# Order of a hybrid mixer's small work: two-source vector forms, parameter rows earlier, weight splits after products, output transposes last, and the first expert pass moved ahead of a gather

## The chip, the cores and the metric

The kernel runs on one core of one Trainium2 chip. The metric is device microseconds of one execution. Its engines are TensorE (PE), VectorE (DVE), ScalarE (ACT), GpSimd (POOL) and SyncE (SP, which issues the large transfers).

## The reference, cut to what matters

One layer of a decoder block for 256 tokens, with 16 learned meta tokens in front (272 rows) and a width of 1024.

```python
h = layer_norm(concat([meta, x]))                      # 272 x 1024
proj = h @ w_in                                        # 1024 x 5640 columns
dn_qkv, dn_z, dn_b, dn_a, sb_qkv, gates = split(proj)
dn_qkv = silu(causal_depthwise_conv(dn_qkv, w))        # 4 heads of 128
beta = sigmoid(dn_b); g = -exp(a_log) * softplus(dn_a + dt_bias)
o_dn = rms_norm(gated_delta_rule_chunked(q, k, v, beta, g)) * silu(dn_z)
o_sb = stick_breaking_attention(sq, sk, sv)            # 8 heads of 64
merged = sig(gA) * (o_dn @ w_branch_dn) + sig(gB) * (o_sb @ w_branch_sb)
h = layer_norm(alpha * h + merged @ w_out)
# MoE: top-1 of 4 groups, top-2 of its 8 experts (32 experts, ff 256)
y = sum over chosen e of combine_e * (silu(h @ gate_e) * (h @ up_e)) @ down_e
return layer_norm(alpha * h + y)[:, 16:]
```

All is float32. The weights are 23 MB of `w_in`, 8 MB of branch and output weights and 96 MB of expert weights (3 MB an expert).

## The kernel before, in words

**The mixer's projection** is 44 groups of 128 columns of `w_in`. `project` runs them in the order of a list: the convolved keys (columns 512 on, groups 0 to 3), the queries and keys of the stick-breaking attention (2056 and 2568 on, groups 4 to 11), the convolved queries (0 on, 12 to 15) and values (1024 on, 16 to 19), the stick-breaking values (3080 on, 20 to 23), z (1536 on, 24 to 27) and the gates (3592 on, 28 to 43). A float32 product is made of three products of rounded halves (`mm3`, L237 to L239): hi with hi, hi with lo, lo with hi. So each group is 8 x 3 matmuls of 128 x 272 or 256, and each weight block is split first (`load_split`): an SP transfer of 0.5 MB into a ring of three raw buffers (L231), a cast on ACT for the hi half (L232), a subtraction on POOL for the lo half (L233; on DVE for three of the first groups) into a ring of WB = 3 buffers of pairs. The activations get the same two halves `hTh` and `hTl` in the first stage (L213 to L217).

**Woven into the groups** are chains of small work, generators that hand over at each `yield`: `delta_net` (the gating numbers beta and g, two chunks' local matrices and a block inversion by doubling, `invert`, then `scan_state` for chunk 0 and chunk 1), `stick_breaking`, the turning of its values, and `parameter_rows`. `weave` takes a step of each chain at a rate per two k-blocks of a group. In the mixer PE and POOL run their instructions in the order in which the program makes them; ACT, DVE and SP are ordered by the tile scheduler. All of them run in order once they are ordered.

In `invert`, for each size n of 4, 8, .., 128 POOL masks a matrix (`mb4c`, .., L488), PE multiplies (`x4c`, L507), ACT casts the result (`xo4c`, L509), and PE goes on with `y4c` and `z4c` (L513, L516). At the end of `scan_state`, the output rows `o` get their norm: sums of squares on ACT (L710), `sso` on DVE (L712 to L714), a power on POOL (L715), one more product on DVE (L716), the scaling on ACT (L718), and then PE transposes them (`poT`, L724) for the branch product.

`parameter_rows` fills `lnr`, `RB` and a selection matrix `self_`: eight POOL instructions (L828 to L835), 12 small transfers on SP (L838), then a scaling on DVE (L839), three casts on ACT (`sel` L840, `RB` L841, `lnh` L842) and a subtraction on DVE (L843). The mixer does not use the result; the second half of the kernel does (L849).

**After the mixer** come the branch products, `w_out`, the layer norm, the router, and 8 units of 4 experts. `gate_up(u)` (L1340) multiplies up to QC slots of each expert, a second pass under `tc.If(most > QC)` takes the rest where an expert has more tokens; `down(u)` (L1389) follows, then the scatter. SP streams the expert weights through rings of buffers: `load_gu` (L889, 2 MB an expert) and `load_dn` (L896, 1 MB an expert). Between the first unit's `gate_up` and its `If` stands the gathering of the second half of the experts' input (`gather(1, ..)` L1195 and `gathered`), and behind the `If` the loads of experts 7 to 10.

Of the kernel before, what the change touches and what calls it, by code (L numbers as in the profile page):

```python
# [19 lines left out]
KT = 8  # L20
# [58 lines left out]
def block_kernel(ctx: ExitStack, tc: tile.TileContext, io, out, dbg=None):  # L79
# [58 lines left out]
    V.memset(one1, 1.0)  # L138
    half = ht.tile([P, HD], F32, name="half")
# [66 lines left out]
    for k in range(KT):  # L206
# [225 lines left out]
    def gating():  # L432
# [6 lines left out]
        V.tensor_scalar_mul(xin[:, 0, :], bb, -1.0)  # L439
# [8 lines left out]
        V.tensor_scalar_add(beta, xin[:, 0, :], 1.0)  # L448
# [3 lines left out]
        V.tensor_scalar_add(zz, u, 2.0)  # L452
# [5 lines left out]
        V.tensor_scalar_mul(poly, z2, 1.0 / 17.0)  # L458
# [3 lines left out]
        V.tensor_scalar_mul(poly, poly, 2.0)  # L462
# [12 lines left out]
        V.tensor_scalar_mul(nedec, dec[:, 0, :], -1.0)  # L475
# [65 lines left out]
    def meta(box):  # L541
# [3 lines left out]
        V.tensor_copy(kTm.rearrange("p (h t) -> p h t", h=HD), qkv[:, 4:8, :NM])  # L545
# [6 lines left out]
        V.tensor_scalar_add(ssm, ssm, RMS_EPS)  # L552
# [31 lines left out]
        V.tensor_copy(vTm.rearrange("p (h t) -> p h t", h=HD), qkv[:, 8:12, :NM])  # L584
# [19 lines left out]
    def local(c, box):  # L604
# [3 lines left out]
        Aall = mx.tile([P, HD, P], F32, name=f"Aall{c}", tag="gtmp", bufs=2)  # L608
# [9 lines left out]
        Es = mx.tile([P, HD, P], F32, name=f"Es{c}", tag="gtmp", bufs=2)  # L618
# [12 lines left out]
        V.tensor_scalar_add(ssk, ssk, RMS_EPS)  # L631
# [24 lines left out]
        V.tensor_scalar(rq, rq, RMS_EPS, float(P), op0=ALU.add, op1=ALU.mult)  # L656
# [15 lines left out]
    def scan_state(c, st, box):  # L672
# [19 lines left out]
        o = mx.tile([P, HD, P], F32, name=f"o{c}", tag="gtmp", bufs=2)  # L692
# [21 lines left out]
        V.tensor_scalar(sso, sso, 1.0 / P, RMS_EPS, op0=ALU.mult, op1=ALU.add)  # L714
# [10 lines left out]
        of = mx.tile([P, HD, P], F32, name=f"of{c}", tag="gtmp", bufs=2)  # L725
# [17 lines left out]
    def delta_net():  # L743
# [80 lines left out]
    def parameter_rows():  # L824

        for _ in range(32):
            yield
# [34 lines left out]
    weave(project(20), (svc, 1.0), (dn, R3), (sbr, R4), (parameter_rows(), 1.0))  # L862
# [272 lines left out]
    load_dn(4, 5)  # L1135
# [315 lines left out]
    def four(u):  # L1451
# [156 lines left out]
```

## Time and profile before

| | us |
|---|---|
| three runs | 544.2, 544.8, 541.4 |
| median | 544.2 |
| profiled execution | 538.66, span 536.9 |
| mean granted TensorE clock in it | 0.922 |

| engine | busy share of the span |
|---|---|
| PE | 86% |
| DVE | 44% |
| ACT | 34% |
| POOL | 32% |

The mixer's 44 groups fill the first 240 us or so of the span, the branches, `w_out`, norms and router lie up to about 300 us, and the experts behind. Up to some 320 us PE is rarely without work and the DMA engines are about half busy; behind it the DMA engines are at their full rate nearly to the end and PE waits for weights now and then. Every row has the start in us (in the time line), the duration, the engine, the line of the kernel, what is written and read, and in square brackets the idle time ahead of it with what ended it. In a table of windows the clock is a share of full speed: 1.00 is 2.4 GHz and 0.50 is 1.2 GHz.

### The profile page before, as it was taken

The numbers are of one execution on the slowest core, as the hardware profiler recorded it, in microseconds if no ns is written. First come the engines' busy times: TensorE is split into PE (matmuls) and PEld (weight loads), VectorE is DVE, ScalarE is ACT, GpSimd is POOL, SyncE is SP. The second block draws the span as 40 slices with busy tenths as digits, with TensorE's granted clock in tenths as the row PEclk, the third lists the DMA queues.
The fourth block names the chain that finished last, engine by engine and source line by source line (L and its number), as shares of the span: only waits on it lengthen the run. The fifth ranks groups of instructions, "written<-read, shape, count | busy, mean of one in ns | idle before, by whom it ended". The sixth has DMA issues, their size and how long they took to land. (4 is left out here: it accounts for less than half of the span.)

```text
span 536.9 us, 8673 instructions
## 1 busy us (share of the span) xinstructions
PE 463.5 (86%) x3301; PEld 328.6 (61%) x3301; DVE 238.2 (44%) x518; ACT 183.9 (34%) x382; POOL 172.7 (32%) x154
## 2 busy tenths in 40 slices
PE   7897999999999978997998888988879888667881
PEld 3697999999997877997876763533222222122330
DVE  5874645665296653039976736120220212110116
ACT  2453546436556365543443312120110202100310
POOL 6594698756544634738132100000000000000002
PEclk9697999999998997999999898889889898878886
DMA  8553344333441612797898958999999999999942
GB/s 210 126 151 86 79 117 109 89 92 108 117 110 49 159 42 78 207 305 270 306 338 336 399 234 336 419 418 418 419 420 420 417 419 418 417 415 419 410 196 79
DMA packets 74581, 136.33 MB, mean 254 GB/s; under 512 B 9857, under 2 KB 59154, under 8 KB 62242
## 3 DMA queue, kind: packets, MB, share of 16 engines
q1 hardware_dynamic: 72640, 134.26, 68.9%
q10 hardware_dynamic: 1890, 1.39, 0.8%
q8 instruction: 32, 0.52, 0.4%
q14 instruction: 19, 0.16, 0.1%
HBM read 133.54 MB, written 2.10 MB: 253 GB/s over the span
## 5 line engine op out<-in xcount | busy, mean ns | idle before, releaser
L233 POOL TENSOR_TENSOR ws_in<-wr_in,ws_in 128x1024 fp32r<-128x1024 f32 x41 | 99.4, 2429 | 64.6 <-ACT ws_in L232 64.3
L237 PE MATMUL pj<-hTh,ws_in 128*128 128x256 f32 (+1 forms) x352 | 109.3, 311 | 1.2 <-DVE hTh L213 0.7
L238 PE MATMUL pj<-hTl,ws_in 128*128 128x256 f32 (+1 forms) x352 | 103.1, 293 | 0.7 <-DVE hTl L217 0.7
L239 PE MATMUL pj<-hTh,ws_in 128*128 128x256 f32 (+1 forms) x352 | 102.6, 292 | 0.0
L1340 PE MATMUL pg<-gu,xs 128*32 128x512 f32 x640 | 77.6, 605 | 8.9 <-DMA gu<-expert_w_up 5.2
L1565 POOL TENSOR_SCALAR rs<-mv 128x1 f32<-128x1 f32 x2 | 0.4, 221 | 229.8 <-DVE mv L1564 229.8
L237 PEld LDWEIGHTS pj<-hTh,ws_in 128*128 128x128 f32 x352 | 69.2, 197 | 3.5 <-issue 1.0
L238 PEld LDWEIGHTS pj<-hTl,ws_in 128*128 128x128 f32 x352 | 69.3, 197 | 1.7 <-DVE hTl L217 1.7
L239 PEld LDWEIGHTS pj<-hTh,ws_in 128*128 128x128 f32 x352 | 69.1, 196 | 0.0
L1389 PE MATMUL py<-dn,hd 128*32 128x512 f32 x320 | 54.1, 802 | 11.9 <-DMA dn<-expert_w_down 6.9
L1340 PEld LDWEIGHTS pg<-gu,xs 128*32 128x32 f32 x640 | 31.0, 111 | 51.0 <-issue 45.5
L232 ACT CAST ws_in<-wr_in 128x1024 fp32r<-128x1024 f32 x44 | 45.9, 1044 | 3.0 <-DMA wr_in<-w_in 3.0
L1393 DVE TENSOR_TENSOR yy<-py,yy 128x512 fp32r<-128x512 f32 x20 | 13.8, 692 | 68.9 <-ACT yy L1392 61.7
L1365 DVE TENSOR_SCALAR sc<-pt,smod 128x256 fp32r<-128x256 f32 x10 | 4.8, 484 | 88.2 <-PE pt L1364 88.2
L1389 PEld LDWEIGHTS py<-dn,hd 128*32 128x32 f32 x320 | 13.2, 138 | 43.8 <-issue 27.2
L1401 PE MATMUL y<-yy,sc 128*128 128x512 f32 x80 | 24.5, 423 | 5.6 <-ACT yy L1392 3.0
L1392 ACT CAST yy<-py 128x512 fp32r<-128x512 f32 x20 | 11.7, 587 | 51.2 <-PE py L1389 51.2
L1401 PEld LDWEIGHTS y<-yy,sc 128*128 128x128 f32 x80 | 13.5, 188 | 22.7 <-ACT yy L1392 7.4
L1371 ACT ACTIVATE gs<-pg 128x256 f32<-128x256 f32 x10 | 3.8, 384 | 68.7 <-PE pg L1340 68.7
L314 DVE SCALAR_TENSOR_TENSOR qkv<-pj,cols,qkv 128x271 f32<-128x271 f32 (+2 forms) x36 | 17.9, 497 | 9.9 <-ACT qkv L312 9.2
L955 POOL TENSOR_TENSOR h<-h,gb 128x512 f32<-128x512 f32 x8 | 12.9, 1643 | 12.9 <-ACT gb L952 12.9
L771 DVE TENSOR_TENSOR_SCAN kp<-kp,one 128x144 f32<-128x144 f32 (+1 forms) x16 | 12.8, 842 | 7.2 <-ACT kp L766 7.2
(535 smaller groups left out, 806.6 us busy)
## 6 DMA issues: line engine op xcount, KB each, us to landing
gu<-expert_w_gate SPq DMA_DIRECT2D x32, 1024.0 KB
gu<-expert_w_up SPq DMA_DIRECT2D x32, 1024.0 KB
dn<-expert_w_down SPq DMA_DIRECT2D x32, 1024.0 KB
wr_in<-w_in SPq DMA_DIRECT2D x44, 512.0 KB
wr_o<-w_out SPq DMA_DIRECT2D x8, 512.0 KB
wr_w_branch_dn<-w_branch_dn SPq DMA_DIRECT2D x4, 512.0 KB
wr_w_branch_sb<-w_branch_sb SPq DMA_DIRECT2D x4, 512.0 KB
h<-x SPq DMA_DIRECT2D x2, 512.0 KB
```

Of the source, the lines that this page charges most:

```text
L232: A.copy(wh, raw)
L233: (sub or V).tensor_sub(wl, raw, f32(wh))
L237: T.matmul(pt, lh, rh, start=first, stop=False)
L238: T.matmul(pt, lh, rl, start=False, stop=False)
L239: T.matmul(pt, ll, rh, start=False, stop=last)
L314: V.scalar_tensor_tensor(y[:, s:], pt[:, :L - s], ccol(3 - s, r + j), y[:, s:], op0=ALU.mult, op1=ALU.add)
L771: V.tensor_tensor_scan(k_, k_, bc(one1, [P, n]), 1.0, op0=ALU.mult, op1=ALU.mult)
L955: G.tensor_tensor(x_, x_, gb, op=op)
L1340: T.matmul(pgd[u, part][c, :], xsd[u, part][:, k, c], raw[e][0][:, :, k, :], start=k == 0, stop=k == KT - 1)
L1389: T.matmul(py[c, :], hd[(u + part) % 2][:, r, c], raw[e][1][:, r, n * 512:(n + 1) * 512], start=r == 0, stop=r == 1)
L1393: V.tensor_sub(yy[:, 1, :], py, f32(yy[:, 0, :]))
L1401: T.matmul(y[t][n], sct[(u + part) % 2][:, t * P:(t + 1) * P], yy[:, p_, :], start=False, stop=p_ == 1 and part == 0 and u == NQ - 1)
```

## The change

1. A helper `with_scalar` writes copies, casts and operations with one scalar as `scalar_tensor_tensor` with a broadcast column of zeros as second source; eleven places of the mixer on DVE use it or a like form with a column of constants. Two copies of 128 x 64 (`kTm`, `vTm`) go from DVE to ACT.
2. `parameter_rows` starts with group 12 and not with group 32. Its POOL instructions and transfers come 20 groups earlier, and 100 yields (25 groups) stand between them and its DVE and ACT instructions, which the scheduler is free to place earlier.
3. `project` makes the split of group i+2 behind the products of group i and not ahead of them.
4. `scan_state` ends with the scaling of `o`; transposing it is a function of its own, `out_turned`, called for both chunks behind the two scans. The ring `gtmp` has three buffers and not two.
5. In the first unit of experts the `If` with the second pass, and the loads of experts 7 to 10, stand ahead of the second half's gathering. A slot buffer of that pass lies in the buffer of expert 5's down weights, whose load moves from ahead of expert 6 to behind expert 7.

```diff
+    def with_scalar(out, x, a, op):
+        V.scalar_tensor_tensor(out, x, a, bc(zero[:x.shape[0]], list(x.shape)) if len(x.shape) == 2 else bc(zero[:x.shape[0], :, None], list(x.shape)), op0=op, op1=ALU.add)
...
-            V.tensor_copy(hTh[:, k, :], hf)
+            with_scalar(hTh[:, k, :], hf, 0.0, ALU.add)
...
+    def splits(n):
+        while len(split) < min(n, len(todo)):
+            c = todo[len(split)][0]
+            split.append(load_split(w_in[:, :, c:c + P], f"in{c}", sub=V if len(split) in DVE_SUB else G))
     def project(n):
         for _ in range(n):
             i = project.i
-            while len(split) < min(i + WB, len(todo)):
-                c = todo[len(split)][0]
-                split.append(load_split(w_in[:, :, c:c + P], f"in{c}", sub=V if len(split) in DVE_SUB else G))
+            splits(i + WB - 1)
...
                 if k == KT - 1:
                     use(pt, j)
+                    splits(i + WB)
...
-        V.tensor_scalar_add(beta, xin[:, 0, :], 1.0)
+        with_scalar(beta, xin[:, 0, :], 1.0, ALU.add)
...
-        V.tensor_copy(kTm.rearrange("p (h t) -> p h t", h=HD), qkv[:, 4:8, :NM])
+        A.copy(kTm.rearrange("p (h t) -> p h t", h=HD), qkv[:, 4:8, :NM])
...
-        V.tensor_scalar(rq, rq, RMS_EPS, float(P), op0=ALU.add, op1=ALU.mult)
+        V.scalar_tensor_tensor(rq, rq, RMS_EPS, bc(pcol, [P, HD]), op0=ALU.add, op1=ALU.mult)
...
         for h in range(HD):
             A.activation(o[:, h, :], o[:, h, :], AF.Copy, scale=sso[:, h:h + 1])
-        yield
-        yield
-        yield
+        os_.append(o)
+        yield
+    os_ = []
+    def out_turned(c):
+        o = os_[c]
         poT = v4(ps("gd", f"poT{c}"))
         for h in range(HD):
             T.transpose(poT[:, h, :], o[:, h, :], ident)
...
         for c in range(2):
             yield from scan_state(c, st, boxes[c])
+            yield
+        for c in range(2):
+            for _ in range(3):
+                yield
+            yield from out_turned(c)
...
     def parameter_rows():
-        for _ in range(32):
-            yield
         G.memset(f32(RB), 0.0)
...
+        for _ in range(100):
+            yield
         V.tensor_scalar(lnr, lnr, asc, None, op0=ALU.mult)
         A.copy(sel, self_)
...
-    weave(project(8), (dn, R1))
+    weave(project(8), (dn, R1), (prow, 1.0))
...
-    load_dn(4, 5)
+    load_dn(4)
...
         gate_up(u)
         if u == 0:
-            for k, tag in ((0, "t"), (2, "y"), (4, "t"), (6, "y")):
-                gather(1, k, tag)
-                ...
+            buffer_dn(5)
         most = nc.values_load(cmi[0:1, u:u + 1], engines=three, min_val=0, max_val=NT)
         with tc.If(most > QC):
             ...
+        n1 = e0 + 7
+        load_gu(n1)
         if u == 0:
+            load_dn(5)
+        if n1 + 4 < NE - 1:
+            load_gu(n1 + 1, n1 + 2, n1 + 3)
+        if u == 0:
+            for k, tag in ((0, "t"), (2, "y"), (4, "t"), (6, "y")):
+                gather(1, k, tag)
+                ...
             rest()
```

How the instructions stand on ACT around group 11 and 12, in the inversion's first doubling steps (`pNc`, `xo4c` are casts of the inversion, `skT` is the copy of a group's result, `ws_in` a weight's hi half). Before:

```order
L232 CAST ws_in128_928<-wr_in128_927 128x1024
L500 CAST pNc1_868<-i0c1_921 128x512
L500 CAST pNm_880<-i0m_939 64x64
L509 CAST xo4c0_955<-x4c0_950 128x512
L509 CAST xo4c1_970<-x4c1_965 128x512
L344 COPY skT_264<-pj2952_932 128x272
L509 CAST xo4m_983<-x4m_981 64x64
```

Now:

```order
L243 CAST ws_in128_981<-wr_in128_980 128x1024
L516 CAST pNc1_869<-i0c1_927 128x512
L516 CAST pNm_886<-i0m_940 64x64
L866 CAST sel_99<-self__100 56x24
L525 CAST xo4c0_956<-x4c0_951 128x512
L525 CAST xo4c1_971<-x4c1_966 128x512
L360 COPY skT_270<-pj2952_933 128x272
L525 CAST xo4m_989<-x4m_987 64x64
L243 CAST ws_in256_1083<-wr_in256_1082 128x1024
L867 CAST RB_96<-lnr_97 24x256
```

The cast `sel` of `parameter_rows` stands directly ahead of `xo4c0`, and the cast of `RB` a few places behind. What `sel` reads, `self_`, is made on POOL, where the eight instructions of `parameter_rows` stand behind the masks `mb8c` and the split of column 128:

```order
L244 TENSOR_TENSOR ws_in2952_881<-wr_in2952_880,ws_in2952_881 128x1024
L504 TENSOR_TENSOR mb4m_888<-mtfm_848,off4_258 64x64
L244 TENSOR_TENSOR ws_in0_923<-wr_in0_922,ws_in0_923 128x1024
L504 TENSOR_TENSOR mb8c0_949<-mtf0_818,off8_259 128x512
L504 TENSOR_TENSOR mb8c1_964<-mtf1_836,off8_259 128x512
L244 TENSOR_TENSOR ws_in128_981<-wr_in128_980,ws_in128_981 128x1024
L504 TENSOR_TENSOR mb8m_985<-mtfm_848,off8_259 64x64
L852 MEMSET RB_96 56x256
L853 MEMSET self__100 56x24
L854 MEMSET lnr_97 56x256
L855 MEMSET asc_101 56x1
L857 AFFINE_SELECT self__100<-self__100 56x24 x2
```

These seven instructions ahead of `RB` are, in another order, all that POOL had between the powers `vs` (L636) and the split of column 256 before, with the masks `mb4c` that stand ahead of the first row here.

On POOL around the norm of chunk 0's output (`sso0`, groups 27 to 30). Before:

```order
L233 TENSOR_TENSOR ws_in3592_1899<-wr_in3592_1898,ws_in3592_1899 128x1024
L233 TENSOR_TENSOR ws_in3720_1986<-wr_in3720_1985,ws_in3720_1986 128x1024
L715 TENSOR_TENSOR sso0_2033<-sso0_2033,mhalf_114 128x4
L233 TENSOR_TENSOR ws_in3848_2060<-wr_in3848_2059,ws_in3848_2060 128x1024
L233 TENSOR_TENSOR ws_in3976_2104<-wr_in3976_2103,ws_in3976_2104 128x1024
```

Now:

```order
L244 TENSOR_TENSOR ws_in3592_1998<-wr_in3592_1997,ws_in3592_1998 128x1024
L731 TENSOR_TENSOR sso0_2065<-sso0_2065,mhalf_120 128x4
L244 TENSOR_TENSOR ws_in3720_2092<-wr_in3720_2091,ws_in3720_2092 128x1024
L244 TENSOR_TENSOR ws_in3848_2136<-wr_in3848_2135,ws_in3848_2136 128x1024
L244 TENSOR_TENSOR ws_in3976_2204<-wr_in3976_2203,ws_in3976_2204 128x1024
```

The split of column 3720, group 29's weights, went behind `sso0`. On PE the transposes `poT0` went from group 29 to group 35 and `poT1` from group 35 to group 38; chunk 1's first product `pkS1` stands in group 29 and not 30, `pvp1` in 30 and not 31, `pqS1` in 31 and not 32.

## Rows read from the trace of the kernel before

**Rows 1.** The page, clock granted to TensorE in 40 slices (tenths).

```profile
PEclk9697999999998997999999898889889898878886
```

**Rows 2.** Waits of PE from 40 to 260 us: total, times, longest.

```profile
PE poT L724 <- ACT o L718: 5.8, 2, 4.6
PE pdc L469 <- DVE gg L464: 3.4, 1, 3.4
PE pvp L685 <- DVE vsc L680: 1.2, 1, 1.2
```

**Rows 3.** Windows, PE alone: window, length, busy (count), clock, DMA share, GB/s.

```profile
46.59:53.41 6.82, 5.87 (x27) 0.50 0.30 78
169.47:172.88 3.41, 3.41 (x18) 0.50 0.34 101
203.60:210.43 6.83, 6.83 (x36) 0.50 0.58 153
```

**Rows 4.** Time line of DVE in the first stage: start, duration, instruction.

```profile
16.12 2.44 DVE L213 CAST hTh<-hf 128x272 fp32r<-128x272 f32 x1
18.60 0.44 DVE L217 TENSOR_TENSOR hTl<-hf,hTh 128x272 fp32r<-128x272 f32 x1
18.95 0.29 DVE L213 CAST hTh<-hf 128x272 fp32r<-128x272 f32 x1
```

**Rows 5.** Groups by line of DVE, 0 to 260 us: busy us, mean ns, idle before.

```profile
L716 DVE TENSOR_TENSOR sso<-sso,rq 128x4 f32<-128x4 f32 x2 | 4.6, 2314 | 2.2 <-POOL sso L715 2.2
...
L656 DVE TENSOR_SCALAR rq<-rq 128x4 f32<-128x4 f32 x2 | 1.6, 792 | 2.7 <-ACT junk L655 2.7
...
L712 DVE TENSOR_TENSOR sso<-sso,rq 128x4 f32<-128x4 f32 x2 | 0.3, 164 | 2.0 <-ACT junk L710 2.0
```

**Rows 6.** Time line of POOL, 62 to 80 us; five rows lie between.

```profile
62.14 2.04 POOL L636 TENSOR_TENSOR vs<-ssk,half 128x4 f32<-128x4 f32 x2 [3.10 <-DVE ssk L631]
...
78.84 0.33 POOL L488 TENSOR_TENSOR mb8m<-mtfm,off 64x64 fp32r<-64x64 f32 x1
```

**Rows 7.** Time line of POOL, 183 to 187 us: `parameter_rows`, first row and `self_`.

```profile
184.05 0.31 POOL L828 MEMSET RB<- 56x256 f32 x1
...
184.66 0.47 POOL L833 TENSOR_SCALAR_AFFINE_SELECT self__100<-self__100 56x24 f32<-56x24 f32 x2
```

**Rows 8.** The inversion's first cast, on ACT, and the product behind it, on PE.

```profile
73.31 0.59 ACT L509 CAST xo4c<-x4c 128x512 fp32r<-128x512 f32 x1 [0.81 <-PE x4c L507]
...
76.25 0.56 PE L513 MATMUL y4c<-xo4c,pTc 128*128 128x128 f32 x4
```

**Rows 9.** Instructions on `lnr` by line: SP's transfers, durations of issue, first and last start.

```profile
L838 SPq DMA_DIRECT2D lnr<-ln_g x4: 259/295/386, 184.7 to 186.4; - x4
...
L838 SPq DMA_DIRECT2D lnr<-ln_emb_b x2: 293/298/303, 189.0 to 189.3; - x2
```

**Rows 10.** POOL's `sso0` with the split behind it; PE's first product of group 29.

```profile
163.98 1.01 POOL L715 TENSOR_TENSOR sso<-sso,mhalf 128x4 f32<-128x4 f32 x1 [5.79 <-DVE sso L714]
164.96 2.38 POOL L233 TENSOR_TENSOR ws_in<-wr_in,ws_in 128x1024 fp32r<-128x1024 f32 x1
...
164.34 0.28 PE L237 MATMUL pj<-hTh,ws_in 128*128 128x256 f32 x1
```

**Rows 11.** PE's `poT1` after its wait, and DVE's last copy that `po2` needs.

```profile
203.04 1.35 PE L724 MATMUL poT<-ident,o 128*128 128x128 f32 x4 [4.59 <-ACT o L718]
...
202.47 0.27 DVE L790 COPY wTm<-pw 64x128 f32<-64x128 f32 x1
```

**Rows 12.** Windows, all engines: the last two numbers are the DMA share and GB/s.

```profile
318.00:324.00 6.00, 5.51 (x41) 4.26 (x34) 2.15 (x5) 1.80 (x4) 0.00 (x0) 1.00 0.00 0
...
326.00:516.00 190.00, 155.64 (x1082) 57.45 (x1081) 29.97 (x81) 29.09 (x65) 0.00 (x0) 0.89 1.01 417
```

**Rows 13.** Time line of PE: the first unit's products, and what follows its `If`.

```profile
311.30 7.44 PE L1340 MATMUL pg<-gu,xs 128*32 128x512 f32 x64 [1.80 <-DMA dn<-expert_w_down]
...
323.33 0.47 PE L849 MATMUL pg1s<-RB,sel 56*128 56x256 f32 x2
```

More of the change, by code (lines that the diff above doesn't have):

```diff
@@ L138, in block_kernel @@
     V.memset(one1, 1.0)
+    zero = ht.tile([P, 1], F32, name="zero")
+    V.memset(zero, 0.0)
+    pcol = ht.tile([P, 1], F32, name="pcol")
+    V.memset(pcol, float(P))
+    ecol = ht.tile([P, 1], F32, name="ecol")
+    V.memset(ecol, RMS_EPS)
+    def with_scalar(out, x, a, op):
+        V.scalar_tensor_tensor(out, x, a, bc(zero[:x.shape[0]], list(x.shape)) if len(x.shape) == 2 else bc(zero[:x.shape[0], :, None], list(x.shape)), op0=op, op1=ALU.add)
     half = ht.tile([P, HD], F32, name="half")
@@ L583, in meta @@
             yield "idle"
-        V.tensor_copy(vTm.rearrange("p (h t) -> p h t", h=HD), qkv[:, 8:12, :NM])
+        A.copy(vTm.rearrange("p (h t) -> p h t", h=HD), qkv[:, 8:12, :NM])
         yield
@@ L607, in local @@
         tag = ("gd", "sb")[c]
-        Aall = mx.tile([P, HD, P], F32, name=f"Aall{c}", tag="gtmp", bufs=2)
+        Aall = mx.tile([P, HD, P], F32, name=f"Aall{c}", tag="gtmp", bufs=3)
         gc = gg[:, 4 * c:4 * c + 4]
@@ L617, in local @@
         A.activation(E, pD, AF.Exp)
-        Es = mx.tile([P, HD, P], F32, name=f"Es{c}", tag="gtmp", bufs=2)
+        Es = mx.tile([P, HD, P], F32, name=f"Es{c}", tag="gtmp", bufs=3)
         V.tensor_mul(Es, E, bc(lt_[:, None, :], [P, HD, P]))
@@ L691, in scan_state @@
             T.matmul(pqS[:, h, :], qT(h)[:, tok], St[:, h, :], start=True, stop=True)
-        o = mx.tile([P, HD, P], F32, name=f"o{c}", tag="gtmp", bufs=2)
+        o = mx.tile([P, HD, P], F32, name=f"o{c}", tag="gtmp", bufs=3)
         for h in range(HD):
@@ L713, in scan_state @@
         V.tensor_mul(sso, sso, rq)
-        V.tensor_scalar(sso, sso, 1.0 / P, RMS_EPS, op0=ALU.mult, op1=ALU.add)
+        V.scalar_tensor_tensor(sso, sso, 1.0 / P, bc(ecol, [P, HD]), op0=ALU.mult, op1=ALU.add)
         G.tensor_tensor(sso, sso, mhalf, op=ALU.pow)
@@ L724, in scan_state @@
             T.transpose(poT[:, h, :], o[:, h, :], ident)
-        of = mx.tile([P, HD, P], F32, name=f"of{c}", tag="gtmp", bufs=2)
+        of = mx.tile([P, HD, P], F32, name=f"of{c}", tag="gtmp", bufs=3)
         V.tensor_mul(of, poT, zT[:, :, c * P:(c + 1) * P])
@@ L853, in block_kernel @@
     svc = sv_turn()
+    prow = parameter_rows()
     weave(project(8), (mk, 0.375), (dn, R1))
-    weave(project(8), (dn, R1))
+    weave(project(8), (dn, R1), (prow, 1.0))
     v_there.append(True)
@@ L861, in block_kernel @@
         S.dma_start(wr[:, :, NG + g * EG:NG + (g + 1) * EG], io["router_expert_w"][g].rearrange("(k p) e -> p k e", p=P))
-    weave(project(20), (svc, 1.0), (dn, R3), (sbr, R4), (parameter_rows(), 1.0))
+    weave(project(20), (svc, 1.0), (dn, R3), (sbr, R4), (prow, 1.0))
+    drain(prow)
     drain(dn)
@@ L894, in load_dn, with buffer_dn @@
             if e < NE:
-                raw[e][1] = unit("rd", f"dn{e}").rearrange("p (r d) -> p r d", r=2)
+                if raw[e][1] is None:
+                    buffer_dn(e)
                 S.dma_start(raw[e][1], io["expert_w_down"][e].rearrange("(p r) d -> p r d", r=2))
+    def buffer_dn(e):
+        raw[e][1] = unit("rd", f"dn{e}").rearrange("p (r d) -> p r d", r=2)
     keep = ctx.enter_context(tc.tile_pool(name="keep", bufs=1, side="right"))
@@ L1231, in slots @@
         e, w = units[u][i], QC
-        if i == 0:
+        if i == 0 and (u, part) == (0, 1):
+            xsd[u, part] = raw[5][1][:, 0, :].rearrange("p (k s) -> p k s", k=KT)
+        elif i == 0:
             xsd[u, part] = f32(lt.tile([P, 1024], F32R, name=f"xs{u}{part}", tag=f"wr{(u + part) % 2 if u + part else 2}").rearrange("p (k s) -> p k s", k=KT))
@@ L1455, in four @@
         if u == 0:
-            for k, tag in ((0, "t"), (2, "y"), (4, "t"), (6, "y")):
-                gather(1, k, tag)
-                for i in range(2):
-                    gathered(1, k + i, A if k % 4 else V)
+            buffer_dn(5)
         most = nc.values_load(cmi[0:1, u:u + 1], engines=three, min_val=0, max_val=NT)
@@ L1464, in four @@
             gate_up(u, 1)
+        n1 = e0 + 7
+        load_gu(n1)
         if u == 0:
+            load_dn(5)
[4 more added lines that the diff above has]
+                gather(1, k, tag)
+                for i in range(2):
+                    gathered(1, k + i, A if k % 4 else V)
             rest()
-        n1 = e0 + 7
-        load_gu(*((n1, n1 + 1, n1 + 2, n1 + 3) if n1 + 4 < NE - 1 else (n1,)))
         if u == 0:
```

14 lines of the change are left out of this document (7 added, 7 removed).

## The prediction

> **What bounds the kernel now.** I read the page's clock and busy lines first. The granted clock is low in a few slices only [rows 1], and PE is busy for most of the first 320 us, so up to there the time is PE's program order: the length of its products, what it waits for, and stretches at 1.2 GHz. The table of PE's waits gives the second thing: between 40 and 260 us only three waits are large, `pdc` 3.4 us, `poT` 5.8 us in two pieces of 1.2 and 4.6, and `pvp` 1.2 us [rows 2]. The windows give the third: behind the 3.4 us gap, the 1.2 us gap and the 4.6 us gap the engine ran at 1.2 GHz for 6.8, 3.4 and 6.8 us [rows 3]. Work at half clock takes twice as long, so about half of such a stretch is lost: 3.4, 1.7 and 3.4 us. From 326 to 516 us the DMA engines are at a share of 1.01 and 417 GB/s, and just ahead of that, from 318 to 324 us, they move nothing [rows 12]: there the time is that of the stream of expert weights, and what counts is when the stream starts again and how many bytes are still to come. All sums below are against the profiled execution's 538.66 us, which lies 5.5 us under the median of 544.2 and under all three runs; differences are then carried to the median.
>
> **Two-source forms.** The six casts of the first stage become two-source operations: 0.44 us in place of 0.29 for the same tile where nothing disturbs them [rows 4], so +0.15 each and up to +0.9 us, since PE's first group waits for these tiles. One of them took 2.44 us while POOL was splitting weights [rows 4]; were the new form free of that, 2.15 us would come back. Which it is, the two products of `sso` tell: the same two-source tile takes 0.16 us in one line and 2.31 us in the other, where POOL's split starts beside it [rows 5]. So two-source operations wait for POOL too, as the one-source form does (0.79 us mean, `rq`) [rows 5]. I take +0.5 us, range -2.2 to +0.9. The gating and norm columns of 128 x 4 or 9 go the same way, at nothing; their cover is that they mostly stand behind other waits. The Trainium skill, "SBUF — State Buffer", section "Who interferes with whom", says that a VectorE instruction with two SBUF inputs contends with a GpSimd instruction that reads SBUF, and the split reads two; by that this part brings no relief, by the opposite view it would bring the 2.15 us. The trace agrees with the page: 2.31 against 0.16 us. The two copies moved to ACT are short and cost nothing as long as ACT keeps its idle share.
>
> **Rows ahead.** This is the largest new term. On ACT the cast `sel` now stands directly ahead of `xo4c0`, and it waits for POOL's `self_`. POOL reaches that behind the same work as before, in another order: from 62.14 to 79.17 us it was busy with the powers `vs`, the masks `mb4` and `mb8` and three splits, and of the seven rows only the first names idle time ahead of it [rows 6]. Then `parameter_rows` needs 184.66 + 0.47 - 184.05 = 1.1 us up to `self_` [rows 7]. So `sel` can't run before about 80.3 us, where `xo4c0` ran at 73.31 [rows 8]. With 0.2 us for `sel` and 0.59 for `xo4c0` [rows 8], `y4c0` starts at 81.1 and not at 76.25 [rows 8]: PE stands for 4.8 us, with everything behind it in program order, group 12's products too. A gap of that size was followed by 6.8 us at 1.2 GHz [rows 2, 3], 3.4 us more. That is +8.2 us; range 3 (PE already late by something else, no half clock) to 11 (the masks, now ahead of a split, wait for the matrix they mask).
>
> The 12 transfers on SP stand between the loads of columns 1024 and 1152; issuing them took from 184.7 to 189.3 + 0.3 = 4.9 us [rows 9]. They can start only when POOL has cleared `lnr`, and `RB`'s cast on ACT waits through DVE for the last; ACT has the first activation of group 12 and `xo8c0` behind it. With PE late by 4.8 us anyhow they land near the time at which these are wanted: +1.0 us, range 0 to 2. What the rows cost at their old place goes away there; it lay in the chain ahead of `poT1`, counted below.
>
> **Splits behind products, chunk 0's norm.** The split of group 29's weights now stands on POOL behind `sso0`. `sso0` started at 163.98 us, and a split behind it at 164.96 for 2.38 us [rows 10]: 167.34 us. PE began group 29 at 164.34 [rows 10]. So PE waits 3.0 us where it found its weights. The 1.2 us wait for `poT0` in that same group [rows 2] goes, and the half clock of 1.7 us follows the one gap as it followed the other: +3.0 - 1.2 = +1.8 us, range -2.9 (no new wait, the old one and its half clock gone) to +3.5 (6.8 us at half clock behind the longer gap). The other groups keep a split ready in the ring; there I take nothing, and a rival below prices the opposite.
>
> **Transposes last.** `pvp1`'s 1.2 us [rows 2] go, since chunk 1's first product comes a group earlier and `vsc1` with it: -1.2, range -1.2 to 0. `poT1`'s 4.59 us [rows 11] go as well, because three groups lie between its scaling and its transposes. Late next is `po2`, which stands right behind the place: its last copy `wTm` was at 202.47 us [rows 11], 4.3 us behind the start of the gap at 203.04 - 4.59 = 198.45. That copy stood on DVE behind the 2.3 us product of `sso` [rows 5] and its wait for POOL of about 1.0 (half of 2.2); without these it ends at some 199.4. So a gap of 1.0 us stays, and behind a gap of that size 3.4 us at half clock: 4.6 - 1.0 + 3.4 - 1.7 = 5.3 us saved, range 0.3 (`po2` as late as before) to 8.0.
>
> **The first unit of experts.** PE ended the first unit's products at 318.74, went through the gathering, and came to what follows the `If` at 323.33 [rows 13]. The loads behind the `If` now come with its new place, 4.6 us earlier, into the stretch in which the DMA engines stood [rows 12]. But expert 5's down weights, 1 MB, move out of the time before into the full stream: 1.05 MB / 417 GB/s = 2.5 us [rows 12]. So the stream ends 2.1 us earlier; I take -1.9, range -4.6 to 0, because a DMA engine that has less to do ahead of the gap can only stand earlier.
>
> **Sum:** 0.5 + 8.2 + 1.0 + 1.8 - 1.2 - 5.3 - 1.9 = +3.1 us, which is 541.8 for a profiled execution and **547 us** beside the median.
>
> **Rivals.**
> *Faster: the wait for `sel` isn't there.* If POOL's work ahead of `self_` shrinks, or PE comes to `y4c0` later by as much, the 8.2 and 1.0 fall out: 547.3 - 9.2 = 538 us. It decides at `xo4c0`: `self_` would have to be there 7 us earlier than the row says. Against it stands a POOL without a gap for 17 us [rows 6]; for it, only that the order of those instructions is new. Within this case the transposes may also give their full 8.0.
> *Slower: POOL's order hurts twice.* `sso1` now stands ahead of a split too, that of column 4360, group 34. If its power starts later than 1.01 + 2.38 = 3.4 us [rows 10] before that group's first product, PE waits as at group 29: 3.0 us and 1.7 to 3.4 for the clock, +4.7 to +6.4, which gives 552 to 554 us. For it: with `sso0` it lies just so. Against: chunk 1's scan has been moved a group earlier.
> *Neither, nearer zero: the two-source forms do free DVE of POOL.* Then the 0.5 turns into -2.2, and about as much comes back at `rq` and `sso`: 543 us. Against it stands the 2.31 us row [rows 5].
>
> **How the numbers follow.** About 1%, or 5.4 us, is what a measurement of this kernel can tell from no change. My forecast, with its own range from 541 to 549.5 us, has 0.40, the two-source relief 0.08, both within 1%. The missing wait at `sel` has 0.21 and lies at faster by over 1%. The double POOL wait has 0.25, and the upper ends of the `sel` wait (11 us) another 0.06, both slower by over 1%. The range reaches from 536 to 555 us: it takes in the most of both outer cases and leaves out the corner of the fast case in which the transposes also give all, and of the slow one in which every gap is followed by the long half clock. So faster 0.21, within 0.48, slower 0.31.
>
> **What the changed kernel's profile would show.** In the table of PE's waits: a new wait of `y4c` for ACT of some 5 us, at about 76 us, with half clock behind it; a wait of group 29's products for POOL's split of about 3 us; no `poT` and no `pvp`; a small one for `po2`. On DVE the cast line's successor beside a split would take over 2 us again. In the windows of the first unit the DMA engines would stand for 8 us as before, but 2 to 3 us earlier in relation to PE's first unit, and start again right behind its products. If `sel` runs without a wait the forecast is wrong to the fast side; if `pj4360` waits for its split, to the slow side; if an early two-source cast beside a running split takes 0.4 us, my reading of the contention is wrong.

## The result and the profile after

The changed kernel takes 545.4 us (median of 20 runs, 543.2 to 548.1) against 540.4 us before (20 runs, 538.4 to 544.8). The ratio is 1.0094, 95% interval 1.0072 to 1.0115: about 5 us, a little slower, inside 1%. Of the three runs shown ahead of the prediction two lay high, so the median before is 540.4 and not 544.2. The profiled execution after took 545.8 us (span 544.1), close to its median; that of before lay 1.7 us under its own, so the two traces differ by 7.1 us. Executions that took over 1.5% more than the fastest of the same kernel are left out of every median and ratio here (two of six in last_undone, two of twelve in forms_back, one of twelve in split_ahead).

The table of PE's waits up to 270 us has these large rows (total, times, longest). They answer to [rows 2]:

```profile
PE y4c L529 <- ACT xo4c L525: 4.0, 1, 4.0
PE pdc L485 <- DVE gg L480: 3.9, 1, 3.9
PE po L831 <- DVE wTm L816: 3.8, 1, 3.8
PE pj L249 <- DVE hTl L228: 3.0, 3, 1.9
...
PE pj L250 <- POOL ws_in L244: 1.6, 2, 1.1
```

`poT` and `pvp` are gone. `y4c` and `po` are new, and together 2.0 us longer than the two `poT` waits. The windows at half clock (window, length, busy, clock, DMA share, GB/s) answer to [rows 3]:

```profile
50.92:57.75 6.83, 6.83 (x34) 0.50 0.18 56
85.05:95.29 10.24, 10.24 (x48) 0.50 0.29 79
211.35:218.17 6.82, 5.45 (x27) 0.50 0.28 77
```

The stretch behind `poT0`'s old wait is gone. Behind the 4.0 us wait of `y4c` TensorE ran 10.24 us at 1.2 GHz, and behind `po`'s 3.8 us again 6.8. ACT's time line shows who held `y4c` (this answers to [rows 8]):

```profile
83.89 0.21 ACT L866 CAST sel<-self__100 56x24 fp32r<-56x24 f32 x1 [7.48 <-POOL self__100 L857]
84.01 1.05 ACT L525 CAST xo4c<-x4c 128x512 fp32r<-128x512 f32 x2
...
91.96 0.41 ACT L867 CAST RB<-lnr 24x256 fp32r<-24x256 f32 x1 [5.57 <-DVE lnr L865]
```

`sel` waited 7.5 us for POOL with the two casts `xo4c` behind it, and `RB` then waited 5.6 us for DVE's scaling of `lnr`, which needs the 12 transfers. POOL's time line around chunk 0's norm answers to [rows 10]:

```profile
175.28 1.01 POOL L731 TENSOR_TENSOR sso<-sso,mhalf 128x4 f32<-128x4 f32 x1 [10.06 <-DVE sso L730]
176.26 4.68 POOL L244 TENSOR_TENSOR ws_in<-wr_in,ws_in 128x1024 fp32r<-128x1024 f32 x2
```

`sso0` came 1.9 us ahead of group 29's start at 177.16 us, and the split behind it 1.1 us too late for that group. DVE's time line around chunk 1's norm; its first row answers to [rows 5]:

```profile
197.60 2.32 DVE L732 TENSOR_TENSOR sso<-sso,rq 128x4 f32<-128x4 f32 x1 [1.19 <-POOL sso L731]
...
202.98 2.96 DVE L797 TENSOR_TENSOR_SCAN kp<-kp,one 128x144 f32<-128x144 f32 x2 [2.72 <-ACT kp L792]
205.86 4.91 DVE L798 TENSOR_TENSOR sg<-sg,kp 128x127 f32<-128x127 f32 x2
```

The product of 128 x 4 took 2.32 us beside a split; two products of the attention's scan took 4.91 us beside two more. These stand ahead of the `wTm` copy that `po2` waits for.

Where the time went is seen best at the start of a group's first product (us, from the time line of PE), here with three kernels of the experiments:

| group | before | after | rows_late | rows_split | best_b |
|---|---|---|---|---|---|
| 1 | 23.6 | 25.6 | 25.5 | 25.6 | 24.9 |
| 12 | 75.4 | 79.6 | 79.5 | 78.9 | 78.8 |
| 13 | 81.1 | 93.3 | 85.2 | 84.6 | 84.5 |
| 28 | 159.9 | 172.7 | 164.0 | 163.4 | 163.3 |
| 30 | 172.5 | 183.9 | 175.2 | 174.5 | 174.4 |
| 34 | 193.2 | 202.4 | 193.7 | 193.1 | 193.0 |
| 36 | 209.6 | 216.7 | 202.9 | 207.3 | 202.2 |
| 43 | 232.2 | 240.2 | 225.7 | 231.3 | 225.0 |

Difference after minus before: +1.9 behind the first stage, +4.2 at group 12, +12.2 at group 13, +12.8 at group 28, then back to +11.3 at 30, +9.2 at 34, +7.1 at 36, and +7.9 at the mixer's end. Group 12 alone lost 8.0 us, groups 12 and 13 together 8.6.

### The profile page after: what moved, and what is told of

Its sections match the earlier page's. It is cut to its first block, busy times and chain, and to the rows that moved or that the text cites. A ratio compares the mean times of both kernels' runs of the same rounds, so it can differ in the third digit from the quotient of the medians.

```text
span 544.1 us, 8672 instructions
## 1 busy us (share of the span) xinstructions
PE 467.0 (86%) x3301; PEld 336.1 (62%) x3301; DVE 237.8 (44%) x519; ACT 184.0 (34%) x384; POOL 170.8 (31%) x154
## 5 line engine op out<-in xcount | busy, mean ns | idle before, releaser
L248 PE MATMUL pj<-hTh,ws_in 128*128 128x256 f32 (+1 forms) x352 | 110.7, 315 | 1.2 <-ACT hTh L227 1.2
L249 PE MATMUL pj<-hTl,ws_in 128*128 128x256 f32 (+1 forms) x352 | 104.6, 297 | 3.0 <-DVE hTl L228 3.0
L250 PE MATMUL pj<-hTh,ws_in 128*128 128x256 f32 (+1 forms) x352 | 104.5, 297 | 1.6 <-POOL ws_in L244 1.6
L1374 PE MATMUL pg<-gu,xs 128*32 128x512 f32 x640 | 80.0, 631 | 8.8 <-DMA gu<-expert_w_up 5.4
L249 PEld LDWEIGHTS pj<-hTl,ws_in 128*128 128x128 f32 x352 | 70.6, 201 | 4.1 <-DVE hTl L228 4.1
L248 PEld LDWEIGHTS pj<-hTh,ws_in 128*128 128x128 f32 x352 | 70.5, 200 | 3.5 <-ACT hTh L227 1.7
L250 PEld LDWEIGHTS pj<-hTh,ws_in 128*128 128x128 f32 x352 | 70.7, 201 | 2.0 <-POOL ws_in L244 2.0
L1374 PEld LDWEIGHTS pg<-gu,xs 128*32 128x32 f32 x640 | 33.9, 115 | 50.5 <-issue 43.0
L1423 PE MATMUL py<-dn,hd 128*32 128x512 f32 x320 | 52.5, 788 | 11.8 <-DMA dn<-expert_w_down 6.9
L1423 PEld LDWEIGHTS py<-dn,hd 128*32 128x32 f32 x320 | 12.5, 136 | 42.9 <-issue 27.4
L330 DVE SCALAR_TENSOR_TENSOR qkv<-pj,cols,qkv 128x271 f32<-128x271 f32 (+2 forms) x36 | 17.9, 497 | 11.3 <-ACT qkv L328 10.7
L1414 ACT COPY hd<-pt 128x256 f32<-128x256 f32 x10 | 3.7, 372 | 32.4 <-PE pt L1413 32.4
```

The source lines that it names most:

```text
L248: T.matmul(pt, lh, rh, start=first, stop=False)
L249: T.matmul(pt, lh, rl, start=False, stop=False)
L250: T.matmul(pt, ll, rh, start=False, stop=last)
L330: V.scalar_tensor_tensor(y[:, s:], pt[:, :L - s], ccol(3 - s, r + j), y[:, s:], op0=ALU.mult, op1=ALU.add)
L1374: T.matmul(pgd[u, part][c, :], xsd[u, part][:, k, c], raw[e][0][:, :, k, :], start=k == 0, stop=k == KT - 1)
L1423: T.matmul(py[c, :], hd[(u + part) % 2][:, r, c], raw[e][1][:, r, n * 512:(n + 1) * 512], start=r == 0, stop=r == 1)
```

## The experiments

All ran beside the kernel before, which took 539.9 to 540.3 us there. "After" has 545.4 us. The ratio comes from the runs side by side and is not quite the quotient of the two medians.

| run | what it is | us | ratio to before (95%) |
|---|---|---|---|
| rows_late | after, part 2 undone | 532.9 | 0.985 (0.981 to 0.990) |
| sel_pool | after, `sel` on POOL | 544.7 | 1.010 (1.007 to 1.013) |
| split_ahead | after, part 3 undone | 542.5 | 1.005 (1.002 to 1.008) |
| forms_back | after, part 1 undone | 543.6 | 1.005 (1.002 to 1.008) |
| last_undone | after, part 4 undone | 546.7 | 1.012 (1.006 to 1.018) |
| moe_back | after, part 5 undone | 545.7 | 1.013 (1.008 to 1.018) |
| sso_pool | after, one product on POOL | 542.5 | 1.004 (1.001 to 1.007) |
| rows_split | after, rows cut in two | 540.3 | 0.998 (0.996 to 1.001) |
| best_b | parts 3, 4, 5 | 530.6 | 0.981 (0.977 to 0.986) |
| best_a | parts 4, 5 | 534.6 | 0.988 (0.985 to 0.991) |
| parts35 | parts 3, 5 | 537.8 | 0.994 (0.990 to 0.997) |
| parts34 | parts 3, 4 | 530.7 | 0.982 (0.979 to 0.985) |

**rows_late**

```diff
-    weave(project(8), (dn, R1), (prow, 1.0))
+    weave(project(8), (dn, R1))
...
+        for _ in range(32):
+            yield
         G.memset(f32(RB), 0.0)
...
-        for _ in range(100):
-            yield
         V.tensor_scalar(lnr, lnr, asc, None, op0=ALU.mult)
```

> The changed kernel with only part 2 undone: parameter_rows at its old place in the last weave. Theory A (the cast `sel` on ACT, waiting for POOL behind the masks and splits, costs most of the loss): the 4.0 us wait of y4c and the 10.2 us at half clock behind it go, 8 to 9 us, so about 537 us where the changed kernel has 545.4, and under the kernel before (540.4). Theory B (POOL's order with the splits behind the products and the two-source forms carry the loss, the wait at y4c would be replaced by another at once): at most 3 us come back, 542.5 or more.

532.9 us: 12.5 us less than after, and 7 less than before. Theory B falls. But it is 4 us more than theory A asked for. The table of groups shows both pieces: 8.0 us in group 12, as expected, and 5.1 us more between groups 34 and 36, where `po2`'s wait has nearly gone. The table of PE's waits has

```profile
PE po L831 <- DVE wTm L816: 0.3, 1, 0.3
```

and the time lines of DVE and of POOL around chunk 1's norm

```profile
188.91 0.16 DVE L732 TENSOR_TENSOR sso<-sso,rq 128x4 f32<-128x4 f32 x1 [1.20 <-POOL sso L731]
```

```profile
188.82 0.30 POOL L854 MEMSET RB<- 56x256 f32 x1
...
190.51 7.65 POOL L244 TENSOR_TENSOR ws_in<-wr_in,ws_in 128x1024 fp32r<-128x1024 f32 x3
```

In this kernel the rows' small POOL instructions (nine of them and not eight: four memsets and five selections) stand between `sso1` and the next split, for 1.7 us. DVE's product runs in that gap in 0.16 us, beside a memset, and not in 2.32 beside a split. The scaling of `o` on ACT, the scores' way out of PSUM behind it and DVE's scans come that much earlier, and the scans meet the splits for less long. That nobody had planned; the next runs test it.

**sel_pool**

```diff
-        A.copy(sel, self_)
+        G.tensor_copy(sel, self_)
```

(the new line directly behind the selections on POOL)

> The changed kernel with one instruction moved: the cast `sel` runs on POOL directly behind the selection that makes `self_`; the casts of RB and lnh stay on ACT. Theory A1 (only `sel` holds ACT): the y4c wait goes and nothing takes its place, 537 to 538 us. Theory A2 (rows ahead as a whole is the trouble: the cast of RB, which stands ahead of xo8c0 on ACT and waits for 12 small transfers that are issued only when POOL has cleared lnr, holds ACT next): no y4c wait, but a wait of y8c for xo8c of some 4 us with half clock behind it, 543 to 546 us.

544.7 us: theory A2. `y4c` waits no more, `y8c` does, since `RB` stands on ACT ahead of `xo8c0`. From the table of PE's waits, and from ACT's time line:

```profile
PE y8c L529 <- ACT xo8c L525: 4.3, 2, 3.6
```

```profile
89.78 0.40 ACT L867 CAST RB<-lnr 24x256 fp32r<-24x256 f32 x1 [9.00 <-DVE lnr L866]
```

So under the 4.0 us wait lay a second one of about the same size. Taking away the cast that the profile names gives nothing that can be measured; what costs is that any cast of the rows stands in ACT's queue here.

**split_ahead**

```diff
-            splits(i + WB - 1)
+            splits(i + WB)
...
                     use(pt, j)
-                    splits(i + WB)
```

> The changed kernel with only part 3 undone: the split of group i+2 ahead of group i again. The scheduler then puts `sel` on ACT behind the xo4 casts and `RB` behind the xo8 casts, and on POOL the splits of columns 2952 and 3720 stand ahead of the masks and of sso0 again. Theory A: the y4c wait goes (at most 1 us is left at y8c), so do the 0.5 and 1.1 us waits for POOL's splits: 8 to 10 us less, 535.5 to 537.5. Theory B' (rows ahead costs ACT its wait wherever the casts stand): a wait of 3 us or more at y8c or y16c and 542 or more.

542.5 us, where theory A asked for 535.5 to 537.5: only in part. `y4c`'s wait is gone, as are those for POOL's splits, but groups 12 to 14 together still lost 6.9 us against before, where they lost 8.6 in after. What is left are two other waits in PE's table, each with half clock behind it (6.83 us behind `pqv`, 10.24 behind `y8c`):

```profile
PE pqv L721 <- DVE vt L702: 2.9, 1, 2.9
...
PE y8c L528 <- ACT xo8c L524: 1.7, 2, 1.4
```

The wait of `y8c` is the rows' again. On ACT `sel` stands ahead of `xo8c` now and waits for POOL as it did ahead of `xo4c` (ACT's time line):

```profile
83.18 0.21 ACT L865 CAST sel<-self__100 56x24 fp32r<-56x24 f32 x1 [5.88 <-POOL self__100 L856]
```

That is the cause which theory B' names, with a shorter wait than its 3 us. `vt` stands on DVE behind two `sg` products that took 4.93 us beside two splits; the expectation missed it.

**forms_back**

```diff
-            with_scalar(hTh[:, k, :], hf, 0.0, ALU.add)
+            V.tensor_copy(hTh[:, k, :], hf)
```

(and the ten other places, with the two copies back on DVE.)

> The changed kernel with only part 1 undone: one-source copies, casts and scalar operations again, kTm and vTm copies on DVE. Theory A: the two-source forms lose 1.0 to 2.5 us in the first stage (the wait for POOL's split only moves from the cast hTh to the subtraction hTl, which now stands ahead of PE's second product) and nothing elsewhere: 543 to 544.5 us. Rival (the forms relieve DVE in the gating and the norms, and the first stage is 2 us longer by chance of the clock's phase): 545.5 to 548 us.

543.6 us, 1.8 less than after; the intervals overlap a little, so the sign is likely and the size open. The trace has 0.6 us at group 1 (24.95 against 25.55) and 0.7 at group 43 (239.5 against 240.2). In after the first-stage rows are the first two, in forms_back the last two:

```profile
16.06 0.43 DVE L148 SCALAR_TENSOR_TENSOR hTh<-hf,zero 128x272 fp32r<-128x272 f32 x1
16.52 3.04 DVE L228 TENSOR_TENSOR hTl<-hf,hTh 128x272 fp32r<-128x272 f32 x1
```

```profile
16.33 0.29 DVE L224 CAST hTh<-hf 128x272 fp32r<-128x272 f32 x1
16.65 2.68 DVE L228 TENSOR_TENSOR hTl<-hf,hTh 128x272 fp32r<-128x272 f32 x1
```

With either form the 2.44 us of [rows 4] moved to the subtraction behind. The form didn't do that: in both kernels part 3 has POOL start the split only at 16.5 to 16.7 us, behind the cast. So the 0.43 us here is not the sign that the prediction named, an early two-source cast beside a running split. Two kernels without part 3 show that case, split_ahead with the new form and best_a, described below, with the old one (DVE's time lines):

```profile
16.11 2.59 DVE L148 SCALAR_TENSOR_TENSOR hTh<-hf,zero 128x272 fp32r<-128x272 f32 x1
```

```profile
15.82 2.49 DVE L224 CAST hTh<-hf 128x272 fp32r<-128x272 f32 x1
```

Whichever instruction meets the split pays, in either form. The new form costs 0.14 us apiece and brings no relief here.

**last_undone**

```diff
         os_.append(o)
         yield
+        yield
+        yield
+        yield from out_turned(c)
...
-        for c in range(2):
-            for _ in range(3):
-                yield
-            yield from out_turned(c)
```

> The changed kernel with only part 4 undone: each chunk's transposes follow its scan at once again, chunk 1 a group later; gtmp keeps three buffers. Theory A (part 4 saves what groups 29 to 36 gained in the trace, 5.7 us): a wait of poT1 for ACT of 3 to 5 us is back with half clock behind it, 549 to 552 us. Rival (part 4 only swaps the wait of poT1 for that of po2, 4.6 against 3.8 us): 545 to 547 us.

546.7 us, 1.3 more than after with overlapping intervals, and in the trace group 43 starts at 239.6 against 240.2: the rival. `po2`'s wait goes and others come in PE's table:

```profile
PE pj L250 <- POOL ws_in L244: 4.5, 3, 2.9
...
PE pvp L701 <- DVE vsc L696: 1.8, 1, 1.8
```

It is not `poT1` that waits, as theory A had it, but group 35's product for its split (2.9 us), which POOL runs behind `sso1`. In the changed kernel part 4 gives little or nothing.

**moe_back**

```diff
         gate_up(u)
         if u == 0:
-            buffer_dn(5)
+            for k, tag in ((0, "t"), (2, "y"), (4, "t"), (6, "y")):
+                ...
...
-    load_dn(4)
+    load_dn(4, 5)
```

> The changed kernel with only part 5 undone: the second half's gathering ahead of the first unit's If and of the loads of experts 7 to 10, expert 5's down weights ahead of expert 6. Theory A (the stream starts 4.4 us earlier but carries 2.5 us more, so 1 to 2 us are saved): 546.4 to 547.5 us. Rival A' (the stream is held up later by buffers that PE frees, so nothing is saved): 545 to 546 us. Rival (the full 4.4 us): 549 us or more.

545.7 us: no difference that can be measured. With an interval of nearly 3 us to either side the times do not tell theory A's 1 to 2 us from nothing. The order itself does as said. In after `gate_up` of the first unit ends at 325.8 us (318.39 + 7.44) and the stream starts again at 327.0; with part 5 undone the unit ends at 325.0 us and the stream stands until 330.5. That is 1.2 us behind the unit and 5.5. Where the gain went is in the windows (the last two numbers are DMA share and GB/s) of after, and behind it of moe_back:

```profile
414.00:430.00 16.00, 14.51 (x122) 4.17 (x116) 1.95 (x5) 2.16 (x5) 0.00 (x0) 0.89 0.90 359
```

```profile
414.00:430.00 16.00, 13.78 (x102) 4.44 (x90) 3.35 (x8) 2.65 (x6) 0.00 (x0) 0.89 1.02 423
```

In after the stream has caught up with PE there: from 405 to 432 us a load of down weights waits 10.1 us for PE's `py`, which frees its buffer, and in moe_back none does. 16 x (1 - 359/423) = 2.4 us are lost, about what the stream had gained after carrying expert 5's weights.

**sso_pool**

```diff
         G.tensor_tensor(sso, sso, mhalf, op=ALU.pow)
-        V.tensor_mul(sso, sso, rq)
+        G.tensor_mul(sso, sso, rq)
```

> The changed kernel with one instruction per chunk moved: the last product of sso with rq runs on POOL behind the power, not on DVE. Theory C (with the rows gone from their old place, POOL starts a 2.4 us split right behind sso1; DVE's product of 128 x 4 then takes 2.3 us, the scaling of o on ACT and what stands behind it there come 2.2 us later, the scans of the attention start later and run beside two splits in a row, and po2 waits 3.8 us for wTm with 6.8 us at half clock): the product takes some 0.2 us on POOL, po2's wait falls to 1.5 us or less and the half clock behind it shrinks or goes, 538.5 to 541.5 us. Rival (the scans collide with splits wherever they start): po2 waits 3 us or more, 544 to 545.5 us.

542.5 us, 2.9 less than after (the intervals touch). The product takes 0.20 us, but `po2` still waits 2.0, between theory C and its rival. POOL's time line and PE's table:

```profile
198.37 0.20 POOL L732 TENSOR_TENSOR sso<-sso,rq 128x4 f32<-128x4 f32 x1
198.52 2.36 POOL L244 TENSOR_TENSOR ws_in<-wr_in,ws_in 128x1024 fp32r<-128x1024 f32 x1
```

```profile
PE po L831 <- DVE wTm L816: 2.0, 1, 2.0
```

The half clock behind it fell to 3.4 us. So the product's wait is about one half of `po2`'s. No run takes the other half apart; in this trace three rows of the attention's scans on DVE ahead of `wTm` took 2.96, 2.80 and 2.75 us, each beside a split.

**rows_split**

```diff
         G.memset(asc, 1.0)
-        for i in (0, 32):
-            G.affine_select(self_, ...)
-        for i, v in ((40, ALPHA), (32, 1.0), (8, ALPHA)):
-            G.affine_select(asc, ...)
...
         for _ in range(100):
             yield
+        for i in (0, 32):
+            G.affine_select(self_, ...)
+        ...
```

> The changed kernel with parameter_rows cut in two: its four memsets and its 12 transfers stay at group 12, the five selections on POOL come behind the 100 yields, and with them, since they read their results, the DVE and ACT instructions. Theory D (rows ahead loses twice: 8 us at y4c because casts stand in ACT's queue, and 4 to 5 us at po2 because POOL's small row instructions no longer stand between sso1 and the next split): no wait of y4c or y8c, but po2 still waits 3 to 4 us with half clock behind it; 536.5 to 538.5 us. Rival D1 (one loss, all of it from the casts): about 533 us and po2's wait under 1 us. Rival D2 (the transfers or memsets at group 12 cost by themselves): 541 us or more.

540.3 us. Theory D in its mechanism: no `y4c` or `y8c` wait, and `po2`'s wait as in after, though memsets and transfers stay early. PE's table and DVE's time line:

```profile
PE po L831 <- DVE wTm L816: 3.8, 1, 3.8
```

```profile
188.27 2.32 DVE L732 TENSOR_TENSOR sso<-sso,rq 128x4 f32<-128x4 f32 x1 [1.19 <-POOL sso L731]
```

The time is 2 us over what was named. One reason is that the rows' casts hold ACT here as well, near the mixer's end. `sel` waits for the late selections, the cast of a weight stands behind it, and so a split comes late and a group waits 1.0 us for it (ACT's time line):

```profile
227.30 0.21 ACT L866 CAST sel<-self__100 56x24 fp32r<-56x24 f32 x1 [2.91 <-POOL self__100 L862]
```

The rest is not explained: at group 43 this trace is almost 9 us ahead of after's, and the median is only 5.1 us lower. By the table of groups the early casts cost 8.0 us in group 12 (after 13.7 us from group 12 to 13, rows_split 5.7), and the missing rows between `sso1` and the split 5.0 between groups 34 and 36 (rows_split 14.2, rows_late 9.2).

**best_b, best_a, parts35 and parts34** undo rows and forms and one more part or none, with the edits shown above.

> Parts 3, 4 and 5 alone: rows at their old place and one-source forms. If the effects add (rows late gave 532.9 where the changed kernel had 545.4; the forms undone gave 1.5 us or, by the first stage in the trace, 0.7): 531 to 532.5 us. If the forms only matter together with the rows ahead: 532.5 to 534.

> Parts 4 and 5 alone: splits ahead of the products, rows late, one-source forms. Theory D: on POOL the split of column 4360 follows sso1 at once again, so DVE's last product of sso takes 2.3 us and po2 waits 2 to 4 us; the 0.5 and 1.1 us waits for POOL's splits and 1.3 us of the first stage go: 532 to 536 us, slower than parts 3, 4 and 5 (530.6). Rival (part 3 is worth nothing or costs): 530 us or less.

> Parts 3 and 5 alone: as the 530.6 us kernel (parts 3, 4 and 5) with part 4 undone. If the transposes-last part is worth what the trace of that kernel shows against the kernel before in groups 34 to 36 (7 us): 536 to 539 us with a wait of poT1 of 3 to 5 us. If it only swaps waits, as it did in the changed kernel: 530 to 532 us.

> Parts 3 and 4 alone: as the 530.6 us kernel with part 5 undone. Theory (4.4 us earlier, 2.5 us more to carry): 532 to 533 us. Rival (nothing, as the changed kernel with part 5 undone left open, 545.7 against 545.4): 530 to 531 us.

best_b beats both kernels: 530.6 us, 1.9% under before (2.3 to 1.4), and just under the range for effects that add. Of the waits that part 4 was made for and of `po2` it has only this in PE's table, and its clock was full from 57 to 288 us:

```profile
PE po L831 <- DVE wTm L816: 0.3, 1, 0.3
```

best_a (splits ahead) is 4.0 us slower, as theory D asked: POOL's split follows `sso1` at once, ahead of the rows, and `po2` waits although the rows stand at their old place. POOL's time line and PE's table:

```profile
186.68 2.36 POOL L244 TENSOR_TENSOR ws_in<-wr_in,ws_in 128x1024 fp32r<-128x1024 f32 x1
188.98 0.30 POOL L853 MEMSET RB<- 56x256 f32 x1
```

```profile
PE po L830 <- DVE wTm L815: 3.9, 1, 3.9
PE pqv L721 <- DVE vt L702: 2.9, 1, 2.9
```

The wait of `pqv` was not expected. Up to group 12 best_a is 2.9 us ahead of best_b (75.9 against 78.8 us), so behind it the kernel loses more than the 4.0 us.

parts35 is 7.2 us slower than best_b: here part 4 is worth what the trace of best_b showed, where it gave little or nothing in the changed kernel. Its waits are not of `poT1` but of a group for its split behind `sso1`, and of `pvp` (PE's table):

```profile
PE pj L250 <- POOL ws_in L244: 5.1, 3, 3.5
PE pvp L701 <- DVE vsc L696: 1.8, 1, 1.8
```

parts34 takes 530.7 us, no difference from best_b that can be measured (the intervals are 1.5 and 2.4 us to either side). Windows of best_b, then of parts34:

```profile
334.00:344.00 10.00, 9.50 (x76) 6.57 (x72) 1.38 (x2) 1.17 (x2) 0.00 (x0) 1.00 0.91 337
```

```profile
334.00:344.00 10.00, 8.46 (x72) 5.73 (x70) 0.88 (x2) 0.38 (x1) 0.00 (x0) 1.00 1.02 418
```

Again the earlier stream slows down later, by 10 x (1 - 337/418) = 1.9 us.

## Why the prediction was right, and where it was not

The forecast was +3.1 us and within 1%; it is +5.0 and within 1%. By terms, read from the two traces, which differ by 7.1 us:

- **Rows ahead, +8.2 and +1.0.** Right in place and cause, and near in sum: groups 12 and 13 lost 8.6 us. The wait was 4.0 us and not 4.8. PE came to `y4c` at 80.6 us and not at 76.25, and POOL had `self_` at 83.9 and not at 80.3; the prediction had counted with neither delay. The half clock behind the wait was 10.24 and not 6.8 us. `RB`'s wait added nothing on top, being hidden under that one, and took its place when that was removed (sel_pool). rows_split shows the 8 us apart from the rest.
- **Transposes last, -5.3: the step that failed.** It took for granted that without `poT1`'s chain and the 2.3 us product of `sso` ahead of it `wTm` would be ready 1.0 us after PE. The norm of chunk 1 had indeed moved ahead, but the split that follows `sso1` held its product for 2.32 us as before, and ACT's and DVE's work behind it ran into two splits in a row. PE waited 3.8 us and not 1.0, with 6.8 us at half clock and not 3.4; between groups 34 and 36 only 2.1 us came back. The prediction counted the rows at their old place as a burden on this chain. In the kernel before POOL ran them at 184.05 us [rows 7], long ahead of `sso1`, and a split followed `sso1` at once (POOL's time line):

```profile
199.20 1.02 POOL L715 TENSOR_TENSOR sso<-sso,mhalf 128x4 f32<-128x4 f32 x1 [6.92 <-ACT wT L788]
200.20 2.33 POOL L233 TENSOR_TENSOR ws_in<-wr_in,ws_in 128x1024 fp32r<-128x1024 f32 x1
```

With parts 3 and 4 `sso1` comes directly ahead of the rows' old place, and there they are a help (`po2` waits 0.3 us in rows_late, 3.8 in rows_split, and 3.9 in best_a, without part 3). Part 2 takes this help away, so it costs 12.5 us in all (rows_late), where the prediction had 9.2.
- **`sso0` ahead of group 29's split, +1.8.** The wait is there, at 1.1 us and not 3.0, and without half clock: `sso0` started 1.9 us ahead of the group (175.28 against 177.16) and not 0.4. Groups 28 to 30 gained 1.5 us. What moved `sso0` earlier was not tried by itself; in the trace no split runs beside the last of the attention's scans ahead of it, which takes 1.06 us, where one stood at 155.39 us before and it took 3.20.
- **Two-source forms, +0.5.** Right in sign and in the reason: they wait for POOL as before (2.59 against 2.49 us) and bring no relief. The first stage lost 1.9 us and not 0.5, because part 3, put at nothing there, costs as much: group 1 starts 1.2 us late with part 3 and the old forms (best_b, 24.9), 1.3 with the new forms and the splits ahead (split_ahead, 24.95), and 0.3 with neither (best_a, 23.9).
- **Splits behind products, the other groups, 0.** A second step that failed, and a miss of about the same size. By group 12 the changed kernel has lost 4.2 us. The three kernels without part 3 start that group at 75.4 to 75.9 us, with the new forms (split_ahead, 75.92) as with the old ones (best_a, 75.87); the eleven with it start it at 77.5 to 80.3. Two kernels that are alike up to there, best_b and parts34, differ by 1.3 us, so the sizes are rough, but most of the 4.2 us goes with part 3. The trace shows a wait of 0.5 us for POOL's split in group 11, where the prediction had a split always ready; the rest is not taken apart.
- **`pvp`, -1.2.** Gone, as said; groups 30 to 33 gained 2.1 us.
- **The first unit of experts, -1.9.** The restart moved by 4.3 us, near the 4.6 said. 2.4 us were lost again where the stream caught up with PE. No gain shows in the times: the end of the range at 0 fits, and the 1.9 us are not excluded.

Of the rivals, the faster one (no wait at `sel`) did not occur: PE came later to `y4c`, as it asked, but POOL did too. Nor did the one in which the two-source forms free DVE of POOL. The slower one (`sso1` holding the split of column 4360 until a group waits) did not occur at that group in the changed kernel; it shows in last_undone and parts35 at the split of column 4488, 2.9 and 3.5 us. That the total lies so close is partly luck. `po2` cost some 3 us more than said, and groups 28 and 29 as much less; up to group 12 3.7 us more were lost than said, and the medians differ by 2.1 us less than the two traces.

Left open: why half clock lasted 10.24 us behind one gap of 4.0 us, and 10.24 us behind one of 1.4 us in split_ahead, against 6.8 us behind 4.6 before and 6.83 behind the same 4.0 us wait of `y4c` in last_undone; what part 3 costs up to group 12; and the size of part 5 below some 3 us.

## What to carry to other kernels

An instruction that nothing needs soon is not free where it is put early: on an engine that runs in order, it holds everything behind it until its own inputs are there, so look at what the scheduler puts behind it, on every engine, and expect a second such instruction under the first. When a piece of work is moved, ask also what will stand beside what without it: a few short instructions between a power and a 2.4 us split were worth 5 us. And judge each part of a combined change alone and together with the others: the transposes last gave 7.2 us in best_b and little or nothing in the changed kernel. Here two parts together gave 1.8% (parts34), one gave nothing that could be measured, and the two others took 2.8% away.

## What the runs showed of the hardware

A VectorE product of 128 x 4 with two SBUF sources took 2.32 us beside a GpSimd subtraction of 128 x 1024 and 0.16 us beside GpSimd memsets, in kernels that differ in little else. The Trainium skill, "SBUF — State Buffer", section "Who interferes with whom", makes that difference: such an instruction contends with a GpSimd instruction that reads SBUF, not with one that only writes. These two rows agree with it. A one-source cast of 128 x 272 on VectorE took 2.49 us beside such a subtraction and its two-source form 2.59, against 0.29 and 0.43 us alone. In the mixer, behind the first stage, a stretch at 1.2 GHz behind a gap was 3.4, 6.8 or 10.24 us long; the longest stood behind gaps of 4.0 and of 1.4 us, and behind the same 4.0 us wait it was 10.24 us in after and 6.83 in last_undone.
